# Reading two column tiles of a projection chunk out of one PSUM bank in a one-layer transformer trunk

## The chip, the core and the metric

One core of a Trainium2 chip runs the kernel. TensorE multiplies (PE in the profile), VectorE (DVE) and ScalarE (ACT) do elementwise work, GpSimd (POOL) small parts of it, and SyncE (SP) issues the weight loads. TensorE writes its results to PSUM, eight banks of 128 partitions x 512 fp32 numbers. The metric is the device time of one execution in microseconds (us). Before the change the three timed runs took 469.76, 470.10 and 471.17 us.

## What is computed

The trunk has one layer for 256 tokens of width 1024: native sparse attention (NSA), a cross attention to 256 memory tokens, a convolutional feed-forward part, each behind an RMS norm with a residual. The change lies in the input projection of the first part:

```python
def nsa_mixer(h, w_in, pe_k, pe_v, ck_w1, ck_w2, cv_w1, cv_w2, w_out):
    q, kc, vc, ks, vs, kw, vw, gl = jnp.split(h @ w_in, cuts, axis=-1)
    ...
    k_cmp = _compress(kv(kc), pe_k, ck_w1, ck_w2)
    v_cmp = _compress(kv(vc), pe_v, cv_w1, cv_w2)
    ...   # 16 heads in 4 groups: compressed, selected and window attention, gated

def _compress(t, pe, w1, w2):      # blocks of 32 tokens, every 16 tokens
    ...
    return jax.nn.gelu(blk @ w1) @ w2
```

`q` has 1024 columns; `kc`, `vc`, `ks`, `kw` have 256 each.

## The kernel before

Every large product is done in pairs of fp32r numbers: a value is split into a high part (`hi`, rounded, on ScalarE) and a low part (`lo`, the rest, on VectorE), and `mm3` (L183 to L185) adds hi x hi, lo x hi and hi x lo in one PSUM bank. Weights come in chunks of 1 MB, each in two halves of 128 x 1024: SyncE loads a half into one of 4 `raw` buffers (L108), ScalarE writes `hi` (L116), VectorE writes `lo` (L120) and by that frees the `raw` buffer. There are 6 `hi` and 6 `lo` buffers. The chunks in order: w_vsvw (numbers 0 and 1), the compressed inputs w_kcvc (2 and 4), w_q (3, 11, 12, 13), w_ks (5), w_ck (6, 7), w_cv (8, 9), w_kw (10), then the memory keys (14 and on).

The front of the kernel (`first`, then `fill`) multiplies the normed input `hT` with these chunks. Each chunk has 256 columns, that is two column tiles of 128, and each tile takes 24 matmuls of 128 x 256 (`proj_ws_steps`). A tile's result fills half a bank, 128 x 256. Before the change each tile has a bank of its own, tagged "proj" or "S" (two banks each), and when its matmuls are done its `out` generator is put on a list that moves a step forward with each matmul group:

- `compress_in(j)`: VectorE multiplies the bank by `row`, the inverse norms (L430); ScalarE and VectorE split it into `c2` (four `c` on each engine for a tile, L188 and L192), and GpSimd copies parts of `c2` (L451, L453).
- `keys(br)`: VectorE multiplies by `row` into a spare part of `xT` (`scaled`, L411); ScalarE writes `KH` twice for each group of heads, VectorE `KL` (L477).
- `queries(ci)`: ScalarE writes half of `QS` (L578), VectorE the other (L584).

`hidden(j)` multiplies `c2` with the compression weights (`pM`, tag "S"), copies the result (`hsb`, L506), turns it by `pH` and computes the gelu; `compressed_keys` splits that into `gh` and `gl` and multiplies them in `pkc`. In the attention behind it, 32 head steps (scores `s`, softmax on VectorE and ScalarE, transposes `pt`, values `O`) are mixed with the last query chunks, the memory keys `pmk` and values `pmv`, and the first output products `pr_out`.

The code gives an order of priority. For TensorE, VectorE and ScalarE a scheduler with a time model makes the final order when the kernel is built; SyncE and GpSimd keep the order of the code.

Of the kernel before, what the change touches and what calls it, by code (L numbers as in the profile page):

```python
# [42 lines left out]
def trunk_kernel(ctx: ExitStack, tc: tile.TileContext, a, out):  # L43
    nc = tc.nc
# [16 lines left out]
    cc = const.tile([P, C_END], F32, name="cc")  # L61
# [118 lines left out]
    def mm3(ps, lw, rx, start, stop):  # L180

        (lh, ll), (rh, rl) = lw, rx
        nc.tensor.matmul(ps, lh, rh, start=start, stop=False)  # L183
        nc.tensor.matmul(ps, lh, rl, start=False, stop=False)  # L184
        nc.tensor.matmul(ps, ll, rh, start=False, stop=stop)  # L185

    def split_hi(hi, src, scale=None):
        nc.scalar.activation(hi, src, AF.Copy, scale=1.0 if scale is None else scale)  # L188

    def split_lo(lo, hi, src, scale=None):  # L190
        if scale is None:
# [79 lines left out]
    def act_pair(nm, tag, pool=act):  # L271
        return tuple(pool.tile([P, KT, S], F32R, tag=f"{tag}_{x}", name=f"{nm}_{x}") for x in ("hi", "lo"))
# [24 lines left out]
    def later(work):  # L297
        running.append(work)
# [19 lines left out]
    done = set()  # L318
# [10 lines left out]
    with tc.tile_pool(name="attn", bufs=1, reuse_waits="tile") as at:  # L329
        KH = at.tile([P, G, 2, 2, P], F32R, name="KH")  # L330
        KL = at.tile([P, G, 2, 2, P], F32R, name="KL")
# [8 lines left out]
        hT = act_pair("hT", "aA")  # L340

        xT = act.tile([P, KT, S], F32, tag="aB_hi", name="xT")
# [40 lines left out]
        QS = at.tile([P, G, HPG, S], F32R, name="QS")  # L383
        with tc.tile_pool(name="cmp", bufs=1, side="right", reuse_waits="tile") as cp:
# [24 lines left out]
            def scaled(ps):  # L409
                v = free.pop(0)  # L410
                nc.vector.tensor_tensor(v, ps[:, :S], row, op=ALU.mult)  # L411
                return v

            NB = 15
            NC = NB * G
            c2 = []

            def compress_in(j):  # L420
                B = [cp.tile([P, 8, 2, 64], F32R, name=f"c2{j}{i}") for i in range(2)]
                pe = cp.tile([P, 2, 8, 1], F32R, name=f"pe{j}")
                o = C_PE + j * 16
                nc.gpsimd.memset(f(B[1][:, :, :, NC + 1:64]), 0.0)
                c2.append(B)

                def out(m, ps):
                    yield from wait("row")
                    v = ps[:, :S]
                    nc.vector.tensor_tensor(v, v, row, op=ALU.mult)  # L430
                    if m == 0:
                        split((B[1][:, :, 0, NC], B[1][:, :, 1, NC], cc[:, o + 8:o + 16]),
                              (pe[:, 0, :, 0], pe[:, 1, :, 0], cc[:, o:o + 8]))
                    yield
                    items = []
                    for gp in range(2):
                        g = 2 * m + gp
                        for par in range(2):
                            v_ = v[gp * 64:gp * 64 + 64].rearrange(
                                "p (n jj r) -> p n jj r", jj=8, r=2)[:, :, :, par]  # L440
                            dh, dl = (B[0][par * 64:par * 64 + 64, :, x, :].rearrange(
                                "p jj (n g) -> p n jj g", g=G)[:, :, :, g] for x in range(2))
# [6 lines left out]
                    if m == 1:  # L449
                        for x in range(2):  # L450
                            nc.gpsimd.tensor_copy(B[1][:, :, x, 0:NC], f(B[0][:, :, x, G:16 * G]))  # L451
                        for x in range(2):
                            nc.gpsimd.tensor_copy(B[0][:, :, x, NC:NC + 1], f(pe[:, x]))  # L453
                        done.add(f"c2{j}")

                for m in range(2):
                    ps = bank(("proj", "S")[m], f"pc{j}{m}")
                    yield from proj_ws_steps(ps[:, :S], c_kv[j], m, hT)
                    later(out(m, ps))


            def keys(br):
                def out(m, ps):
                    yield from wait("row")
                    v = scaled(ps)
                    yield
                    items = []
                    for gp in range(2):
                        g = 2 * m + gp
                        own = slice(gp * 64, gp * 64 + 64)  # L470
                        oth = slice(64 - gp * 64, 128 - gp * 64)
                        v_ = v[own].rearrange("p (h k) -> p h k", h=2)
                        split_hi(KH[own, g, :, br, :], v_)
                        items.append((KH[own, g, :, br, :], KL[own, g, :, br, :], KH[oth, g, :, br, :], v_))
# [12 lines left out]
            gel = cp.tile([P, 2, 2, NC], F32, name="gel")  # L487
# [46 lines left out]
            for g in range(G):  # L534
                z = slice(64, 128) if g % 2 == 0 else slice(0, 64)
# [36 lines left out]
            def queries(ci):  # L572
                pr = ci // 2

                def out(i, ps):
                    for gp in range(2):
                        own = slice(gp * 64, gp * 64 + 64)
                        nc.scalar.activation(QS[own, 2 * pr + gp, i, :], ps[own, :S], AF.Copy, scale=0.125)  # L578
                    yield
                    for gp in range(2):  # L580
                        g = 2 * pr + gp
                        own = slice(gp * 64, gp * 64 + 64)
                        oth = slice(64 - gp * 64, 128 - gp * 64)
                        nc.vector.scalar_tensor_tensor(QS[oth, g, i, :], ps[own, :S], 0.125,  # L584
                                                       f(QS[own, g, i, :]), op0=ALU.mult,
                                                       op1=ALU.subtract)
# [362 lines left out]
    with tc.tile_pool(name="cross", bufs=1, reuse_waits="tile") as cr:  # L949
# [61 lines left out]
        for t in range(NT):  # L1011
            for ci in range(EARLY):
                ps = bank("proj", f"pcq{t}{ci}")
# [4 lines left out]
                for c in range(2):  # L1018
                    o = c * S + t * P
# [20 lines left out]
    with tc.tile_pool(name="ffn", bufs=1, reuse_waits="tile") as fp:  # L1040
# [8 lines left out]
        for t in range(NT):  # L1049
            for fi in range(FIRST):  # L1050
                ps = bank("proj", f"upt{t}{fi}")
# [4 lines left out]
                for gv_ in range(2):  # L1056
                    o = gv_ * S + t * P
# [158 lines left out]
```

## Time and profile before

| | us |
|---|---|
| median of 3 timed runs (lowest to highest) | 470.10 (469.76 to 471.17) |
| the profiled execution | 470.6 |
| its span, first to last instruction | 468.5 |
| TensorE busy | 449.5 |
| VectorE busy | 326.8 |
| ScalarE busy | 293.9 |
| GpSimd busy | 37.6 |

Busy times are of one profiled execution. Times within it count from the span's first instruction. A matmul's row lasts longer than the distance to the next one, since matmuls overlap: the pace is read from the starts. "Idle before" is the time that an engine stood still before an instruction, with what released it. The mean clock of TensorE over the whole execution was 0.986 of 2.4 GHz.

### The profile page before, as it was taken

To read this page: it belongs to the slowest core of one execution; us is meant where nothing else is said; L and a number is where in the kernel's file an instruction comes from. 1 tells how busy PE (TensorE), PEld (TensorE's weight loads), DVE (VectorE), ACT (ScalarE), POOL (GpSimd) and SP (SyncE) were. 2 spreads that over 40 slices of the span, in tenths; PEclk is the share of its full clock that TensorE was granted. 3 is DMA by queue.
4 is the path that set the end of the run, shared out by engine and by line. 5 is a ranking of instruction groups with operands and counts; after the bars stand their busy time and mean duration, and the time that the engine had idled before them with its cause. 6 is when DMAs were issued, how large, how long until landed. Compare 5 with 4: busy or idle time off the path is not lost.

```text
span 468.5 us, 8741 instructions
## 1 busy us (share of the span) xinstructions
PE 449.5 (96%) x3278; PEld 415.1 (89%) x3278; DVE 326.8 (70%) x716; ACT 293.9 (63%) x613; POOL 37.6 (8%) x82
## 2 busy tenths in 40 slices
PE   7999796999999999999999999999999999999994
PEld 3899695899999777899998899999999999888984
DVE  4779968688978697666455466987877777645413
ACT  5778858766778688675464466866555556534301
POOL 4122200301100000010000010000000000000103
PEclk8999988999999999999999999999999999999998
DMA  7986687434332201547325274755555555554402
GB/s 257 365 277 217 214 252 280 156 118 150 97 104 77 92 1 41 186 140 236 120 91 166 86 241 124 239 184 182 184 185 187 182 187 184 199 191 149 148 0 91
DMA packets 22074, 77.05 MB, mean 164 GB/s; under 512 B 2704, under 2 KB 3088, under 8 KB 22032
## 3 DMA queue, kind: packets, MB, share of 16 engines
q1 hardware_dynamic: 21312, 74.65, 48.1%
q10 hardware_dynamic: 720, 1.84, 1.2%
q8 instruction: 26, 0.43, 0.4%
q14 instruction: 16, 0.13, 0.1%
HBM read 75.43 MB, written 1.05 MB: 163 GB/s over the span
## 4 chain that ended last, share of the span: by engine, by line
PE 83%; DVE 6%; DMA 6%; ACT 2%; issue 2%; POOLq 0%; DVEq 0%; SPq 0%; POOL 0%; ACTq 0%
PE up L185 8%; PE up L184 8%; PE up L183 8%; PE pd L184 4%; PE pd L183 4%; PE pd L185 4%; DMA raw<-in_w_q 3%; DVE lo L120 3%; PE O L832 2%; PE pt L810 2%; PE pmk L183 2%; PE pcq L183 2%; PE pmk L184 2%; PE pmv L184 2%; PE pmv L183 2%
## 5 line engine op out<-in xcount | busy, mean ns | idle before, releaser
L120 DVE TENSOR_TENSOR lo<-raw,hi 128x1024 fp32r<-128x1024 f32 x134 | 164.0, 1229 | 67.8 <-ACT hi L116 66.9
L116 ACT ACTIVATE hi<-raw 128x1024 fp32r<-128x1024 f32 x134 | 141.6, 1059 | 64.4 <-PE pd L185 17.7
L183 PE MATMUL up<-h_hi,hi 128*128 128x256 f32 x304 | 86.2, 283 | 0.0
L185 PE MATMUL up<-h_hi,lo 128*128 128x256 f32 x304 | 86.1, 283 | 0.0
L184 PE MATMUL up<-h_lo,hi 128*128 128x256 f32 x304 | 86.1, 283 | 0.0
L183 PEld LDWEIGHTS up<-h_hi,hi 128*128 128x128 f32 x304 | 58.4, 192 | 0.0
L184 PEld LDWEIGHTS up<-h_lo,hi 128*128 128x128 f32 x304 | 58.4, 192 | 0.0
L185 PEld LDWEIGHTS up<-h_hi,lo 128*128 128x128 f32 x304 | 58.4, 192 | 0.0
L185 PE MATMUL pd<-hi,aT_lo 128*128 128x512 f32 (+1 forms) x110 | 38.5, 350 | 0.0
L184 PE MATMUL pd<-lo,aT_hi 128*128 128x512 f32 (+1 forms) x110 | 38.4, 349 | 0.0
L183 PE MATMUL pd<-hi,aT_hi 128*128 128x512 f32 (+1 forms) x110 | 38.4, 349 | 0.0
L796 ACT ACTIVATE pp<-pp,nm 128x128 f32<-128x128 f32 (+1 forms) x64 | 28.5, 447 | 6.1 <-DVE nm L790 5.4
L790 DVE CUSTOM_DVE_ANT_0 pp<-s,tri,nrs 128x128 f32<-128x128 f32 (+1 forms) x64 | 24.0, 413 | 5.2 <-PE pt L810 3.3
L185 PEld LDWEIGHTS pd<-hi,aT_lo 128*128 128x128 f32 x110 | 20.7, 188 | 3.0
L184 PEld LDWEIGHTS pd<-lo,aT_hi 128*128 128x128 f32 x110 | 20.7, 188 | 2.9
L183 PEld LDWEIGHTS pd<-hi,aT_hi 128*128 128x128 f32 x110 | 20.7, 188 | 2.9
L1076 ACT ACTIVATE th<-c 128x256 f32<-128x256 f32 x22 | 9.1, 414 | 22.2 <-DVE c L1074 22.2
L814 ACT ACTIVATE pT<-pt 128x256 f32<-128x256 f32 (+1 forms) x32 | 15.3, 485 | 11.2 <-PE pt L810 11.0
L183 PE MATMUL pq<-hT_hi,hi 128*128 128x256 f32 x64 | 19.0, 297 | 0.4 <-DVE QS L584 0.4
L185 PE MATMUL pq<-hT_hi,lo 128*128 128x256 f32 x64 | 19.0, 296 | 0.0
L184 PE MATMUL pq<-hT_lo,hi 128*128 128x256 f32 x64 | 18.9, 295 | 0.0
L804 DVE TENSOR_SCALAR pp<-pp,den 128x128 f32<-128x128 f32 (+1 forms) x64 | 18.4, 327 | 0.6
(305 smaller groups left out, 1146.7 us busy)
## 6 DMA issues: line engine op xcount, KB each, us to landing
raw<-in_w_up SPq DMA_DIRECT2D x44, 512.0 KB, 4.3
raw<-in_w_dn SPq DMA_DIRECT2D x20, 512.0 KB, 4.3
raw<-in_w_q SPq DMA_DIRECT2D x8, 512.0 KB, 6.1
raw<-in_w_mk SPq DMA_DIRECT2D x8, 512.0 KB, 5.0
raw<-in_w_mv SPq DMA_DIRECT2D x8, 512.0 KB, 3.8
raw<-in_w_out SPq DMA_DIRECT2D x8, 512.0 KB, 3.8
raw<-in_ca_wq SPq DMA_DIRECT2D x8, 512.0 KB, 4.5
raw<-in_ca_wo SPq DMA_DIRECT2D x8, 512.0 KB, 4.1
```

Source lines behind the costliest of these rows:

```text
L116: nc.scalar.activation(his[i][h], raws[i][h], AF.Copy)
L120: nc.vector.tensor_tensor(t, raws[i][h], f(his[i][h]), op=ALU.subtract)
L183: nc.tensor.matmul(ps, lh, rh, start=start, stop=False)
L184: nc.tensor.matmul(ps, lh, rl, start=False, stop=False)
L185: nc.tensor.matmul(ps, ll, rh, start=False, stop=stop)
L790: nc.vector.tensor_tensor_reduce(self.ppv[:, br], sv[:, br], tri[:, 1 - t:], nrs[:, t:t + 1], 3e38, ALU.add, ALU.min, self.nm[:, br:br + 1])
L796: nc.scalar.activation(self.ppv[:, br], self.ppv[:, br], AF.Exp, bias=self.nm[:, br:br + 1], scale=-1.0, accum_out=self.den[:, br:br + 1])
L804: nc.vector.tensor_scalar(self.ppv[:, br], self.ppv[:, br], den[:, br:br + 1], None, op0=ALU.mult)
L810: nc.tensor.transpose(self.pt[:, o:o + P], self.pp[:, o:o + P], ident)
L814: nc.scalar.activation(self.pT[:, :self.w], self.pt[:, :self.w], AF.Copy)
L832: nc.tensor.matmul(O[r:r + DK, m * P:(m + 1) * P], V[:, blk // 2, blk % 2, g, :], group[i].pT[:, blk * P:(blk + 1) * P], start=False, stop ...
L1076: nc.scalar.activation(th, c, AF.Tanh, scale=0.5)
```

## The change

A chunk's two column tiles now go into the two halves of one bank, and `out` runs once for the chunk, behind the second tile, on both halves: the compressed inputs are multiplied by `row` in one 128 x 512 instruction and split in four double `c` on each engine; the keys take a 512 wide part of `xT` at once; `KH`, `KL` and `QS` are written for both tiles in one instruction. The banks of the compressed inputs and the keys now all have the tag "S", those of the queries "proj". Multiplications and weights stay the same.

```diff
-            free = [xT[:, k] for k in range(1, KT)] * 2
+            free = [xT[:, k:k + 2] for k in (2, 4)]
...
-                def out(m, ps):
+                def out(ps):
                     yield from wait("row")
-                    v = ps[:, :S]
-                    nc.vector.tensor_tensor(v, v, row, op=ALU.mult)
...
+                    both = ps.rearrange("p (m s) -> p m s", m=2)
+                    nc.vector.tensor_tensor(both, both, row.unsqueeze(1).to_broadcast([P, 2, S]), op=ALU.mult)
...
+                ps = bank("S", f"pc{j}")
                 for m in range(2):
-                    ps = bank(("proj", "S")[m], f"pc{j}{m}")
-                    yield from proj_ws_steps(ps[:, :S], c_kv[j], m, hT)
-                    later(out(m, ps))
+                    yield from proj_ws_steps(ps[:, m * S:(m + 1) * S], c_kv[j], m, hT)
+                later(out(ps))
...
-                    v = scaled(ps)
+                    v = free.pop(0)
+                    nc.vector.tensor_tensor(v.rearrange("p a s -> p (a s)"), ps,
+                                            row.unsqueeze(1).to_broadcast([P, 2, S]), op=ALU.mult)
...
+                ps = bank("S", f"pk{br}")
                 for m in range(2):
-                    ps = bank(("S", "proj")[m], f"pk{br}{m}")
-                    yield from proj_ws_steps(ps[:, :S], c_ks if br == 0 else c_kw, m, hT)
-                    later(out(m, ps))
+                    yield from proj_ws_steps(ps[:, m * S:(m + 1) * S], c_ks if br == 0 else c_kw, m, hT)
+                later(out(ps))
...
-                        nc.scalar.activation(QS[own, 2 * pr + gp, i, :], ps[own, :S], AF.Copy, scale=0.125)
+                        nc.scalar.activation(QS[own, 2 * pr + gp, i:i + 2, :], both[own], AF.Copy, scale=0.125)
...
+                ps = bank("proj", f"pq{ci}")
                 for ct in range(2):
-                    ps = bank("proj", f"pq{ci}{ct}")
-                    yield from proj_ws_steps(ps[:, :S], c_q[ci], ct, hT)
-                    later(out((ci % 2) * 2 + ct, ps))
+                    yield from proj_ws_steps(ps[:, ct * S:(ct + 1) * S], c_q[ci], ct, hT)
+                later(out((ci % 2) * 2, ps))
```

The scheduler gives the three compute engines another order up to the end of the attention. VectorE has 714 rows of work in the old program and 690 in the new, ScalarE 531 and 507, TensorE 3154 in both. SyncE's and GpSimd's orders stay the same. In the lists `lo5_0` is the low part of the first half of chunk 5; before the change `pq11` is the second tile of query chunk 1, and after it `pq2` is the whole of query chunk 2.

VectorE from the first half of w_ks (chunk 5) to w_ck (chunk 6), before:

```order
L120 TENSOR_TENSOR lo5_0_367<-raw5_0_360,hi5_0_362 128x1024
L584 SCALAR_TENSOR_TENSOR QS_238<-pq00_359,QS_238 64x256 x2
L192 TENSOR_TENSOR c200_254<-pc00_258,c200_254 64x16x8 x4
L430 TENSOR_TENSOR pc11_507<-pc11_507,xT_102 128x256
L120 TENSOR_TENSOR lo5_1_385<-raw5_1_378,hi5_1_380 128x1024
L192 TENSOR_TENSOR c200_254<-pc01_333,c200_254 64x16x8 x4
L210 SCALAR_TENSOR_TENSOR sq_mem0b_1082,ss_mem0b_1081<-mem0_1045 128x512
L192 TENSOR_TENSOR c210_462<-pc11_507,c210_462 64x16x8 x4
L120 TENSOR_TENSOR lo6_0_476<-raw6_0_467,hi6_0_469 128x1024
```

After:

```order
L120 TENSOR_TENSOR lo5_0_366<-raw5_0_359,hi5_0_361 128x1024
L120 TENSOR_TENSOR lo5_1_384<-raw5_1_377,hi5_1_379 128x1024
L192 TENSOR_TENSOR c200_254<-pc0_258,c200_254 64x2x16x8 x4
L210 SCALAR_TENSOR_TENSOR sq_mem0b_1031,ss_mem0b_1030<-mem0_999 128x512
L120 TENSOR_TENSOR lo6_0_461<-raw6_0_452,hi6_0_454 128x1024
L580 SCALAR_TENSOR_TENSOR QS_238<-pq0_358,QS_238 64x512 x2
L120 TENSOR_TENSOR lo6_1_481<-raw6_1_474,hi6_1_476 128x1024
L120 TENSOR_TENSOR lo7_0_531<-raw7_0_517,hi7_0_519 128x1024
```

The second half of w_ks follows the first, the two products of the second input are gone from here, and `QS` comes behind the first half of w_ck.

TensorE around the first matmul of `pkc`, before:

```order
L184 MATMUL pq11_965<-hT_lo_101,hi11_1_780 128x256
L185 MATMUL pq11_965<-hT_hi_100,lo11_1_784 128x256
L183 MATMUL pkc_850<-gh_816,w2h_820 128x60
L183 MATMUL pq20_1019<-hT_hi_100,hi12_0_799 128x256
L184 MATMUL pq20_1019<-hT_lo_101,hi12_0_799 128x256
```

After:

```order
L185 MATMUL pq2_973<-hT_hi_100,lo12_1_804 128x256
L183 MATMUL pq2_973<-hT_hi_100,hi12_1_796 128x256
L183 MATMUL pkc_817<-gh_783,w2h_787 128x60
L184 MATMUL pq2_973<-hT_lo_101,hi12_1_796 128x256
L185 MATMUL pq2_973<-hT_hi_100,lo12_1_804 128x256
```

Before, `pkc` stood between query chunks 1 and 2; now it stands behind 19 matmuls of chunk 2's first tile.

TensorE at the scores of head 17 (`s200`), before:

```order
L779 MATMUL s200_1841<-KH_92,QS_238 128x256
L780 MATMUL s200_1841<-KL_93,QS_238 128x256
L183 MATMUL pmv11_2357<-hi19_0_1850,memT_hi_1009 128x256
L184 MATMUL pmv11_2357<-lo19_0_1874,memT_hi_1009 128x256
L185 MATMUL pmv11_2357<-hi19_0_1850,memT_lo_1010 128x256
```

After:

```order
L775 MATMUL s200_1785<-KH_92,QS_238 128x256
L776 MATMUL s200_1785<-KL_93,QS_238 128x256
L185 MATMUL pmv11_2301<-hi19_1_1854,memT_lo_964 128x256
L183 MATMUL pr_out00_2427<-hi20_0_1993,oT_hi_965 128x512
L184 MATMUL pr_out00_2427<-lo20_0_2004,oT_hi_965 128x512
L185 MATMUL pr_out00_2427<-hi20_0_1993,oT_lo_966 128x512
```

Before, the memory values (`pmv11`) still had 18 matmuls to go at head 17; now one is left, and the output products (`pr_out00`) begin there.

## Rows read from the trace of the kernel before

**Rows 1.** The page: span, and part 1, busy time of each engine.
```profile
span 468.5 us, 8741 instructions
PE 449.5 (96%) x3278; PEld 415.1 (89%) x3278; DVE 326.8 (70%) x716; ACT 293.9 (63%) x613; POOL 37.6 (8%) x82
```

**Rows 2.** Stretches: busy us (instructions) per engine, granted clock, DMA share, GB/s.
```profile
30.00:40.00 10.00, 10.00 (x86) 10.00 (x86) 9.15 (x20) 9.73 (x21) 2.81 (x7) 1.00 0.74 251
40.00:50.00 10.00, 10.00 (x86) 10.00 (x85) 9.79 (x19) 8.72 (x18) 1.46 (x3) 1.00 0.80 248
50.00:60.00 10.00, 6.39 (x48) 5.58 (x47) 9.09 (x15) 7.41 (x13) 1.15 (x2) 0.99 0.66 210
60.00:70.00 10.00, 10.00 (x73) 10.00 (x73) 6.74 (x13) 5.70 (x8) 0.00 (x0) 0.84 0.82 240
70.00:80.00 10.00, 5.56 (x35) 5.28 (x34) 8.01 (x17) 8.61 (x21) 0.00 (x0) 0.84 0.80 304
148.00:160.00 12.00, 12.00 (x90) 10.34 (x91) 7.65 (x34) 7.50 (x20) 0.00 (x0) 1.00 0.31 108
160.00:182.00 22.00, 20.70 (x168) 16.30 (x165) 20.18 (x106) 19.04 (x70) 0.22 (x1) 1.00 0.00 1
```

**Rows 3.** TensorE in order of time: start, us, work, [idle before <- releaser].
```profile
46.53 0.28 PE L499 MATMUL pM<-hi,c 128*128 128x256 f32 x1
...
59.39 0.44 PE L510 MATMUL pH<-ident,hsb 128*128 128x128 f32 x2 [1.95 <-ACT hsb L506]
...
71.95 0.28 PE L184 MATMUL pq<-hT_lo,hi 128*128 128x256 f32 x1
72.07 0.28 PE L185 MATMUL pq<-hT_hi,lo 128*128 128x256 f32 x1
76.43 0.30 PE L183 MATMUL pkc<-gh,w2h 128*128 128x60 f32 x1 [4.08 <-ACT gh L188]
77.09 0.55 PE L183 MATMUL pq<-hT_hi,hi 128*128 128x256 f32 x1 [0.36 <-DVE QS L584]
```

**Rows 4.** VectorE in order of time, 30 to 42 us.
```profile
30.60 1.23 DVE L120 TENSOR_TENSOR lo<-raw,hi 128x1024 fp32r<-128x1024 f32 x1 [0.36 <-ACT hi L116]
...
35.03 1.23 DVE L120 TENSOR_TENSOR lo<-raw,hi 128x1024 fp32r<-128x1024 f32 x1
...
37.79 0.69 DVE L210 SCALAR_TENSOR_TENSOR sq_mem0b<-mem 128x512 bf16<-128x512 f32 x1
...
40.18 2.36 DVE L120 TENSOR_TENSOR lo<-raw,hi 128x1024 fp32r<-128x1024 f32 x2
```

**Rows 5.** SyncE: its longest wait in total (us, times, longest); three weight loads.
```profile
SPq L108 <- DVE lo L120: 204.2, 75, 29.4
...
36.28 0.33 SPq L108 DMA_DIRECT2D raw<-in_w_ck  x1
...
41.43 0.33 SPq L108 DMA_DIRECT2D raw<-in_w_cv  x1
...
54.68 10.77 SPq L108 DMA_DIRECT2D raw<-in_w_q  x6
```

**Rows 6.** ScalarE in order of time, before `gh`.
```profile
72.73 1.06 ACT L116 ACTIVATE hi<-raw 128x1024 fp32r<-128x1024 f32 x1 [1.17 <-DMA raw<-in_w_q]
73.69 1.70 ACT L188 ACTIVATE KH<-xT 64x256 fp32r<-64x256 f32 x4
```

**Rows 7.** By line and form: count, busy us, mean ns, idle; VectorE, then ScalarE.
```profile
L584 DVE SCALAR_TENSOR_TENSOR QS<-pq,QS 64x256 fp32r<-64x256 f32 x16 | 6.8, 422 | 3.1 <-ACT QS L578 2.9
L192 DVE TENSOR_TENSOR c<-pc,c 64x128 fp32r<-64x128 f32 x16 | 6.3, 391 | 0.4 <-ACT c L188 0.2
L936 DVE TENSOR_TENSOR x_sb<-pr_wo,x_sb 128x512 f32<-128x512 f32 x4 | 2.7, 687 | 5.1 <-PE pr_wo L185 5.1
...
L578 ACT ACTIVATE QS<-pq 64x256 fp32r<-64x256 f32 x16 | 6.0, 375 | 1.1 <-PE pq L185 0.9
L708 ACT ACTIVATE sT<-pst 64x512 f32<-64x512 f32 x4 | 2.4, 588 | 0.3 <-PE pst L702 0.3
```

More of the change, by code (lines that the diff above doesn't have):

```diff
@@ L407, in rms @@
                 nc.gpsimd.tensor_scalar(hrs, rs_x, 0.5, None, op0=ALU.mult)
[L409 to L412, printed above, removed]
             NB = 15
@@ L425, in compress_in @@
                 c2.append(B)
-                def out(m, ps):
+                def out(ps):
                     yield from wait("row")
-                    v = ps[:, :S]
-                    nc.vector.tensor_tensor(v, v, row, op=ALU.mult)
-                    if m == 0:
-                        split((B[1][:, :, 0, NC], B[1][:, :, 1, NC], cc[:, o + 8:o + 16]),
-                              (pe[:, 0, :, 0], pe[:, 1, :, 0], cc[:, o:o + 8]))
+                    both = ps.rearrange("p (m s) -> p m s", m=2)
+                    nc.vector.tensor_tensor(both, both, row.unsqueeze(1).to_broadcast([P, 2, S]), op=ALU.mult)
+                    split((B[1][:, :, 0, NC], B[1][:, :, 1, NC], cc[:, o + 8:o + 16]),
+                          (pe[:, 0, :, 0], pe[:, 1, :, 0], cc[:, o:o + 8]))
                     yield
@@ L436, in out @@
                     for gp in range(2):
-                        g = 2 * m + gp
                         for par in range(2):
-                            v_ = v[gp * 64:gp * 64 + 64].rearrange(
-                                "p (n jj r) -> p n jj r", jj=8, r=2)[:, :, :, par]
+                            v_ = ps[gp * 64:gp * 64 + 64].rearrange(
+                                "p (m n jj r) -> p m n jj r", m=2, jj=8, r=2)[:, :, :, :, par]
                             dh, dl = (B[0][par * 64:par * 64 + 64, :, x, :].rearrange(
-                                "p jj (n g) -> p n jj g", g=G)[:, :, :, g] for x in range(2))
+                                "p jj (n m gp) -> p m n jj gp", m=2, gp=2)[:, :, :, :, gp] for x in range(2))
                             items.append((dh, dl, v_))
@@ L448, in out @@
                         split_lo(lo, hi, v_)
[L449 to L454, printed above, removed]
+                    for x in range(2):
+                        nc.gpsimd.tensor_copy(B[1][:, :, x, 0:NC], f(B[0][:, :, x, G:16 * G]))
+                    for x in range(2):
+                        nc.gpsimd.tensor_copy(B[0][:, :, x, NC:NC + 1], f(pe[:, x]))
+                    done.add(f"c2{j}")
+                ps = bank("S", f"pc{j}")
                 for m in range(2):
-                    ps = bank(("proj", "S")[m], f"pc{j}{m}")
-                    yield from proj_ws_steps(ps[:, :S], c_kv[j], m, hT)
-                    later(out(m, ps))
+                    yield from proj_ws_steps(ps[:, m * S:(m + 1) * S], c_kv[j], m, hT)
+                later(out(ps))
             def keys(br):
-                def out(m, ps):
+                def out(ps):
                     yield from wait("row")
-                    v = scaled(ps)
+                    v = free.pop(0)
+                    nc.vector.tensor_tensor(v.rearrange("p a s -> p (a s)"), ps,
+                                            row.unsqueeze(1).to_broadcast([P, 2, S]), op=ALU.mult)
                     yield
@@ L468, in out @@
                     for gp in range(2):
-                        g = 2 * m + gp
                         own = slice(gp * 64, gp * 64 + 64)
                         oth = slice(64 - gp * 64, 128 - gp * 64)
-                        v_ = v[own].rearrange("p (h k) -> p h k", h=2)
-                        split_hi(KH[own, g, :, br, :], v_)
-                        items.append((KH[own, g, :, br, :], KL[own, g, :, br, :], KH[oth, g, :, br, :], v_))
+                        v_ = v[own].rearrange("p m (h k) -> p m h k", h=2)
+                        hi, lo, copy = (z[r].rearrange("p (m gp) h b k -> p m gp h b k", gp=2)[:, :, gp, :, br]
+                                        for z, r in ((KH, own), (KL, own), (KH, oth)))
+                        split_hi(hi, v_)
+                        items.append((hi, lo, copy, v_))
                     yield
@@ L575, in out @@
                 def out(i, ps):
+                    both = ps.rearrange("p (i s) -> p i s", i=2)
                     for gp in range(2):
                         own = slice(gp * 64, gp * 64 + 64)
-                        nc.scalar.activation(QS[own, 2 * pr + gp, i, :], ps[own, :S], AF.Copy, scale=0.125)
+                        nc.scalar.activation(QS[own, 2 * pr + gp, i:i + 2, :], both[own], AF.Copy, scale=0.125)
                     yield
@@ L583, in out @@
                         oth = slice(64 - gp * 64, 128 - gp * 64)
-                        nc.vector.scalar_tensor_tensor(QS[oth, g, i, :], ps[own, :S], 0.125,
-                                                       f(QS[own, g, i, :]), op0=ALU.mult,
+                        nc.vector.scalar_tensor_tensor(QS[oth, g, i:i + 2, :], both[own], 0.125,
+                                                       f(QS[own, g, i:i + 2, :]), op0=ALU.mult,
                                                        op1=ALU.subtract)
+                ps = bank("proj", f"pq{ci}")
                 for ct in range(2):
-                    ps = bank("proj", f"pq{ci}{ct}")
-                    yield from proj_ws_steps(ps[:, :S], c_q[ci], ct, hT)
-                    later(out((ci % 2) * 2 + ct, ps))
+                    yield from proj_ws_steps(ps[:, ct * S:(ct + 1) * S], c_q[ci], ct, hT)
+                later(out((ci % 2) * 2, ps))
             def compressed_keys():
```

## Prediction

> **What bounds the kernel now.** I read the page first: the profiled execution spans 468.5 us and TensorE is busy for 449.5 of them [rows 1]. So nearly all of the span is matmul time, the change removes no matmul, and only TensorE's idle time and its slow stretches can be won. Next the table of stretches, to see where those lie [rows 2]. From 30 to 50 us TensorE is busy throughout, from 50 to 60 it is busy for 6.39 us, from 70 to 80 for 5.56, and in 60 to 70 and 70 to 80 the granted clock averages 0.84. A mean of 0.84 over 10 us is 3.2 us at the lower of the two levels, 1.2 GHz, which throws away up to 1.6 us of matmul work each time. So about 8 us of idle time and up to 3 us of slow clock lie between 50 and 80 us, exactly the stage that the change rewrites. Everything after 190 us keeps its order.
>
> Then the two large waits of TensorE [rows 3]. One ends at 59.39 (1.95 us, the copy `hsb`). The other starts behind the matmul of 72.07 and ends at 76.43: 4.08 us, until ScalarE has written `gh`, the high part of the compressed keys' hidden layer, which `pkc` multiplies. Behind `pkc` the third query chunk then waits 0.36 us more, for VectorE to empty the bank (`QS`).
>
> Why is `gh` late? On ScalarE it stands behind four `KH` copies, and these behind a split that waited 1.17 us for the last half of w_q to land [rows 6]. That load left SyncE late: the six w_q halves go out between 54.68 and 65.45, and what SyncE waits for is VectorE's `lo`, 204.2 us in total [rows 5], because a `raw` buffer is free only when `lo` has read it. VectorE's rows show the same link from its side: `lo` of 35.03 ends at 36.26 and a load leaves at 36.28; the first `lo` of 40.18 ends at 41.4 and a load leaves at 41.43 [rows 4, 5]. VectorE is busy for 9.15, 9.79 and 9.09 us of each 10 from 30 to 60 [rows 2]. So VectorE's queue paces the weights here, and TensorE pays at 50 to 80.
>
> **The change part by part.** *Fewer, larger instructions.* By the order, VectorE and ScalarE lose 24 instructions each: 2 row products of the compressed inputs, 8 `c` splits, 2 products for the keys, 4 `KL` and 8 `QS` on VectorE; 8 `c`, 8 `KH` and 8 `QS` on ScalarE. Two 64x256 `QS` on VectorE cost 2 x 0.422 = 0.844, and the nearest form of twice the size, 128x512 from a bank, 0.687: 0.157 saved for each instruction removed. On ScalarE 2 x 0.375 - 0.588 = 0.162 [rows 7]. So 24 x 0.157 = 3.8 us and 24 x 0.162 = 3.9 us go from the two queues. The strided `c` splits in double size are not in the trace: one costs at least the 0.391 of the single one and at most two of them, 0.78; I take 2 x 0.391 - 0.157 = 0.63.
>
> The Trainium skill (Perfetto Trace Analysis, Optimizing Scalar/DVE Operations) gives smaller overheads, about 125 ns for VectorE on PSUM and 60 on SBUF; the rows' 0.157 is used. By these figures the 20 removed instructions on PSUM and 4 on SBUF are worth an estimated 2.7 us, and the forecast below would be some 0.5 us higher.
>
> *VectorE's order.* The `lo` of the second w_ks half now stands right behind the first. It can end at 30.60 + 2 x 1.23 = 33.06 instead of 36.26, so its buffer's load leaves 3.2 us earlier [rows 4, 5]. The next `lo` has four double `c` (2.5 us) and a 0.69 square ahead of it and ends at 33.06 + 2.5 + 0.7 + 1.2 = 37.5 instead of 41.4. The lead then shrinks: the second input's `c` splits now come all four together behind the second memory square, and `KL` moves ahead of a `lo`. Adding durations down both queues in the new order, the six w_q loads leave between 0.5 and 2.2 us earlier. Nothing earlier than that can reach `gh`; if the transfers themselves set the pace (0.80 of the DMA engines' time in 70 to 80 [rows 2]), it is 0. I take **1.6 us**, the later w_q halves being nearer the upper end.
>
> *TensorE's order at `pkc`.* The third query chunk has its own bank now, so it needn't wait for the second chunk's bank, and 19 of its matmuls stand ahead of `pkc`. They run at 0.12 us each (71.95 to 72.07 [rows 3]): 19 x 0.12 = **2.3 us** of work that fills the wait. In the old order that chunk waited for the bank alone behind `pkc`, not for weights. The **0.4 us** wait for the bank goes as well. If the cover is gone, because TensorE arrives late by as much as `gh` is early, the 1.6 us is lost but the 2.3 stays.
>
> *Bank sharing.* The five tiles pc, pk, pM now all take turns in two banks. `pM0` started at 46.53 [rows 3]; its bank is that of the second compressed input, whose last split I put at 47.0 by the same addition. That is a wait of about 0.5 us, and 2 us if the second memory square, which stands ahead of the splits on ScalarE, gets its load late. TensorE still has 3.6 us of idle time to come in 50 to 60 [rows 2] behind it, on weights that don't depend on `pM0`, so I cost it at nothing. One step stands against me there: `pH1` now follows two matmuls that need the first w_q half. That wait may grow by some 2 us, but 12 more matmuls (1.4 us) are done before it.
>
> *The attention's order.* The scheduler moved this too. The memory projections (288 matmuls) fill gaps between the heads; before head 17's scores 270 of them stood, now 287, and with transposes 21 more instructions in all. At 0.12 us that is 2.5 us of TensorE's work taken out of the second half of the heads, where only the softmax engines are left to set the pace. From 148 to 160 VectorE is busy 7.65 of 12 us, from 160 to 182 20.18 of 22 [rows 2]: idle 4.35 and 1.82. The softmax can move up into the first, hardly in the second. Bounds: nothing is lost, or all 2.5. I take half, **1.2 us**.
>
> **Sum:** 2.3 + 0.4 + 1.6 - 1.2 = 3.1, say 3 us off a span of 468.5. The profiled execution took 470.6 us in all and the three timed runs have a median of 470.1, 0.5 below it. So 470.1 - 3.0 = **467.1 us**.
>
> **The rivals.**
>
> *More.* If TensorE no longer comes to a standstill at `pkc`, the second stretch at half clock (1.6 us) may go too, and the heads may give nothing back: 2.3 + 0.4 + 1.6 + 1.6 = 5.9, less some waiting left over, 464.6. For it: the clock fell only behind the two large waits. Against: I still see up to 2.3 us of wait.
>
> *Given back.* The softmax engines set the pace from head 17 on, and w_q is early by only 0.5: 2.3 + 0.4 + 0.5 - 2.5 = 0.7, which is 469.4. For it: 20.18 of 22 us.
>
> *The shared bank.* `pM0` waits 2 us for the second input's splits and everything behind them on ScalarE and VectorE is late with it, so that w_q gains nothing: 2.3 + 0.4 - 1.2 = 1.5, which is 468.6. Against: the idle time that follows takes most of it. The Trainium skill (Perfetto Trace Analysis, Matmuls) says that independent groups should rotate through banks so that emptying one overlaps the next; this rival is what that rule would do here.
>
> *Slower.* In the tail without projections TensorE stands still between heads and its clock falls. Before, 160 to 182 holds only 1.3 us of its idle time and the clock stays at 1.00 [rows 2]. With 2.5 us less of its work between the heads, a pause like the one that ended at 59.39 [rows 3], behind which the clock fell, becomes possible. Each costs 1.6 us as above; two of them give 2.3 + 0.4 + 0.5 - 2.5 - 3.2 = -2.5, which is 472.6. It decides from the second such pause on, since with one the sum is -0.9. Against: 20.7 of 22 us are busy there now.
>
> That the change doesn't do what it says can be ruled out: the order shows the double forms and the counts.
>
> **How the numbers follow.** Forecast 0.50, more 0.17, given back 0.15, shared bank 0.07, slower 0.11. A measurement of this kernel tells about 0.3% from no change, which is 1.4 us. The forecast with its own spread (465.6 to 468.9) and "more" give faster 0.68; "given back" and most of the shared bank are the same, with the forecast's upper edge 0.21; slower 0.11. The range from 464.5 to 470.4 takes in everything but the slower case and the far end of "more".
>
> **What would show it.** In the profile after: VectorE's double forms near 0.69 and the `c` form near 0.63; the `lo` that ended at 36.26 ending near 33; the w_q loads leaving 0.5 to 2.2 us earlier; no wait of the third query chunk for `QS`, and a wait of TensorE at `pkc` under 2.3 us; first scores about 3 to 4 us earlier, and the attention's end about 3 us earlier. If the waits at 50 to 80 us shrink and the total doesn't move, my tail term is wrong; if `pkc` comes no earlier than 76 us, the DMA and not VectorE paced w_q.

## The result and the profile after

Four runs of the changed kernel took 463.66 to 464.90 us, median 463.88, beside a median of 469.93 for the kernel before: a ratio of 0.989, 95% interval 0.987 to 0.991. By the medians it is faster by 6.0 us, by the ratio by 5.2 (4.1 to 6.3), where 3.0 was forecast, and the median lies 0.6 us below the low end of the range. Six more runs of the same kernel in a later measurement, below, gave 465.76 and 0.993 (0.990 to 0.995), which is inside the range. So the change is worth some 3.5 to 6 us.

The profiled execution after took 463.8 us. First the page: the span, and the busy time of each engine.

```profile
span 461.9 us, 8682 instructions
PE 445.3 (96%) x3278; PEld 411.5 (89%) x3278; DVE 325.1 (70%) x692; ACT 289.0 (63%) x589; POOL 41.8 (9%) x82
```

TensorE is busy for 4.2 us less than in [rows 1] with the same 3278 matmuls. No matmul was removed, so most of this is matmul time that ran at the lower clock before: the two stretches at 0.84 in [rows 2] make up to 3.2 us of it (2 x 0.16 x 10). The table of stretches (columns as in [rows 2]) shows where:

```profile
40.00:50.00 10.00, 8.21 (x67) 7.83 (x66) 9.27 (x16) 6.54 (x11) 2.50 (x4) 1.00 0.63 204
50.00:60.00 10.00, 8.76 (x73) 8.36 (x72) 8.68 (x13) 7.72 (x13) 0.00 (x0) 1.00 0.78 244
60.00:70.00 10.00, 10.00 (x86) 10.00 (x85) 6.84 (x12) 5.22 (x7) 0.00 (x0) 1.00 0.91 299
70.00:80.00 10.00, 8.34 (x70) 8.14 (x70) 8.56 (x17) 9.85 (x22) 0.00 (x0) 1.00 0.51 197
...
90.00:100.00 10.00, 8.95 (x67) 7.75 (x65) 8.42 (x26) 5.90 (x14) 3.41 (x4) 1.00 0.36 122
...
160.00:182.00 22.00, 20.68 (x141) 16.35 (x140) 18.89 (x77) 18.00 (x51) 0.22 (x1) 1.00 0.10 29
```

The granted clock was 0.84 in two of these stretches before; now it is 1.00 in all. From 70 to 80 us TensorE gets 70 matmuls done where it got 35. TensorE in order of time (start, duration, work, [idle before <- releaser]), its three largest waits and what stands ahead of `pkc`:

```profile
47.91 0.36 PE L494 MATMUL pM<-hi,c 128*128 128x256 f32 x1 [1.45 <-DVE c L192]
...
71.38 0.28 PE L183 MATMUL pq<-hT_hi,hi 128*128 128x256 f32 x1
73.31 0.29 PE L183 MATMUL pkc<-gh,w2h 128*128 128x60 f32 x1 [1.66 <-ACT gh L188]
73.45 0.36 PE L184 MATMUL pq<-hT_lo,hi 128*128 128x256 f32 x1
...
91.24 0.70 PE L244 MATMUL pb_mem<-dg_mem 128*128 128x256 f32 x2 [1.05 <-POOL dg_mem L243]
```

The stop at `pkc` is 1.66 us instead of 4.08 [rows 3], chunk 2 is at work on both sides of it, and its wait for `QS` is gone. Two new stops stand there: `pM0` waits 1.45 us for the last split of the bank that it shares, and `pb_mem` 1.05 us for GpSimd. Both matter below.

### The profile page after: what moved, and what is told of

The parts are those of the page before. It is cut to its first block, busy times and chain, and to the rows that moved or that the text cites. A ratio compares the mean times of both kernels' runs of the same rounds, so it can differ in the third digit from the quotient of the medians.

```text
span 461.9 us, 8682 instructions
## 1 busy us (share of the span) xinstructions
PE 445.3 (96%) x3278; PEld 411.5 (89%) x3278; DVE 325.1 (70%) x692; ACT 289.0 (63%) x589; POOL 41.8 (9%) x82
## 3 DMA queue, kind: packets, MB, share of 16 engines
HBM read 75.43 MB, written 1.05 MB: 166 GB/s over the span
## 4 chain that ended last, share of the span: by engine, by line
PE 89%; DVE 4%; DMA 2%; ACT 1%; POOL 1%; issue 1%; POOLq 0%; DVEq 0%; SPq 0%; ACTq 0%
PE up L183 8%; PE up L185 8%; PE up L184 8%; PE pd L185 4%; PE pd L183 4%; PE pd L184 4%; PE O L828 3%; PE pt L806 2%; DVE lo L120 2%; PE pcq L183 2%; PE pmv L185 2%; PE pmv L184 2%; PE pmv L183 2%; PE pcq L185 2%; PE pcq L184 2%; PE pr_out L183 2%
## 5 line engine op out<-in xcount | busy, mean ns | idle before, releaser
L184 PE MATMUL pmv<-lo,memT_hi 128*128 128x256 f32 x64 | 18.7, 292 | 0.0
L183 PE MATMUL pmk<-memT_hi,hi 128*128 128x256 f32 x64 | 18.2, 285 | 0.2 <-DVE QS L580 0.2
```

## Where the time went: one table for all kernels

Executions start differently: the first matmul of `pc` came at 21.00 us in the profiled run before, at 20.23 after, and between 19.31 and 22.62 in the others. What the kernels do to the time is therefore counted from that matmul, between starts in the trace: to the first matmul of `pkc` that reads `gh`, from there to the last of `pq`, and on to the last of `pr_out`. Behind that all take 263.6 us to the last matmul, but for two with 264.0 and 264.1.

| kernel (label) | ratio to before, 95% interval | to `pkc` | to last `pq` | to last `pr_out` | sum |
|---|---|---|---|---|---|
| before | | 55.43 | 17.66 | 104.56 | 177.65 |
| after | 0.989 (0.987 to 0.991) | 53.09 | 12.87 | 105.87 | 171.83 |
| after_again | 0.993 (0.990 to 0.995) | 53.27 | 12.87 | 107.39 | 173.53 |
| q_only | 0.988 (0.984 to 0.992) | 52.82 | 12.95 | 105.37 | 171.14 |
| c_only | 0.998 (0.996 to 1.001) | 55.63 | 16.60 | 103.89 | 176.12 |
| a_q2 | 1.000 (0.998 to 1.002) | 55.25 | 18.71 | 104.56 | 178.52 |
| a_c2 | 0.990 (0.988 to 0.993) | 53.04 | 12.88 | 105.85 | 171.77 |
| small | 0.995 (0.993 to 0.997) | 58.50 | 12.48 | 104.53 | 175.51 |
| q20S | 0.998 (0.996 to 1.001) | 54.17 | 18.35 | 104.15 | 176.67 |
| fill6 | 0.998 (0.996 to 1.001) | 54.74 | 16.87 | 104.57 | 176.19 |
| rot | 0.992 (0.988 to 0.995) | 55.14 | 15.88 | 105.09 | 176.11 |
| b_ghv | 0.997 (0.995 to 0.998) | 52.24 | 18.98 | 104.14 | 175.35 |
| a_ghv | 0.988 (0.985 to 0.992) | 52.97 | 12.66 | 105.30 | 170.93 |
| q_ghv | 0.987 (0.984 to 0.989) | 51.36 | 13.99 | 105.48 | 170.83 |

So of the 6.6 us between the two profiled spans 0.8 is the start, and 5.8 the change: 2.3 to `pkc`, 4.8 behind it, and 1.3 given back in the attention.

My theory then (A): TensorE no longer stops at `pkc`, it has work there and keeps its clock. The rival (B): the lighter queues of VectorE and ScalarE gain in proportion to the instructions removed.

## Experiments: which part of the change

**q_only**, the kernel before with the queries part alone:

```diff
...
+                ps = bank("proj", f"pq{ci}")
                 for ct in range(2):
-                    ps = bank("proj", f"pq{ci}{ct}")
-                    yield from proj_ws_steps(ps[:, :S], c_q[ci], ct, hT)
-                    later(out((ci % 2) * 2 + ct, ps))
+                    yield from proj_ws_steps(ps[:, ct * S:(ct + 1) * S], c_q[ci], ct, hT)
+                later(out((ci % 2) * 2, ps))
```

> The kernel before with the queries part alone: both column tiles of a query chunk in one bank, QS written in half as many instructions (8 fewer on VectorE, 8 on ScalarE). By the order, 18 matmuls of query chunk 2 stand ahead of the first pkc matmul here, as after the whole change. Theory A (the gain comes from TensorE no longer stopping at pkc: 19 x 0.12 us of work moved ahead, the bank wait gone, and the clock not falling behind the stop): most of the whole change's 6 us, 464 to 466.5 us, and a granted clock of 1.00 in 70 to 80 us. Theory B (the gain is the lighter VectorE and ScalarE queues, in proportion to the instructions removed, 8 of 24): 6 x 8/24 = 2.0 us, 468 us, and the stop at pkc stays over 3 us.

It took 462.84 us, less than theory A's range: the whole gain, by a third of the removed instructions.

**a_q2**, the reverse: the kernel after with this part undone.

> The kernel after with the queries part undone: each query tile again has a bank of its own and QS is written per tile; compressed inputs and keys stay merged. By the order, no matmul of query chunk 2 stands ahead of pkc. Theory A: 468 to 469.5 us, the wait at pkc over 3 us and the half clock behind it back. Theory B: 16 of 24 removed instructions stay removed, 6 x 16/24 = 4 us, 465.9 us.

It took 469.28 us, ratio 1.000: nothing is gained by the other two parts, though 32 of the 48 instructions stay removed. **c_only**, the compressed inputs alone:

> The kernel before with the compressed inputs part alone: one bank for a chunk's two tiles, one row product and four double splits (10 fewer instructions on VectorE, 8 on ScalarE). By the order, no matmul of query chunk 2 stands ahead of pkc, as before the change. Theory A: the stop at pkc and the half clock behind it stay, so at most the 0.5 to 1.6 us by which gh comes earlier: 468.3 to 469.5 us, clock 0.84 in one of the stretches 60 to 80. Theory B: 6 x 10/24 = 2.5 us, 467.4 us.

468.19 us, and the interval includes no change. **a_c2**, the kernel after with the compressed inputs undone:

> The kernel after with the compressed inputs part undone: queries and keys stay merged, the compressed inputs are again multiplied and split per tile in banks of their own (proj and S). By the order, 18 matmuls of query chunk 2 stand ahead of pkc. If the order at pkc and the clock carry the gain: 462.5 to 464.5. If the gain goes with the number of removed instructions: 10 of 24 less on VectorE, 469.5 - 3.4 = 466.1.

465.44 us, above the first case's range and nearer to the second's 466.1, so that the time decides nothing here; the stages are those of after to 0.1 us, and in this profile the first `pc` came 2.0 us later than in after's. Theory B falls with q_only (462.84, it had 468) and a_q2 (469.28, it had 465.9). TensorE at `pkc` in q_only, then in a_q2, and a_q2's stretch from 70 to 80 us:

```profile
72.48 0.29 PE L183 MATMUL pkc<-gh,w2h 128*128 128x60 f32 x1 [1.37 <-ACT gh L188]
```
```profile
74.56 0.42 PE L183 MATMUL pkc<-gh,w2h 128*128 128x60 f32 x1 [5.07 <-ACT gh L188]
...
70.00:80.00 10.00, 5.20 (x24) 5.10 (x24) 8.37 (x18) 9.84 (x21) 0.00 (x0) 0.70 0.55 218
```

a_q2's TensorE comes to `pkc` early, stops for 5.07 us, and goes on at half clock. Its lighter queues did bring w_q sooner (ScalarE starts on the last half 50.69 us behind the first `pc`, 51.73 before), but ScalarE's order spends that again. ScalarE in a_q2:

```profile
70.01 1.06 ACT L116 ACTIVATE hi<-raw 128x1024 fp32r<-128x1024 f32 x1 [1.90 <-DMA raw<-in_w_q]
70.97 2.56 ACT L188 ACTIVATE KH<-xT 64x512 fp32r<-64x512 f32 x4
73.43 0.75 ACT L573 ACTIVATE QS<-pq 64x256 fp32r<-64x256 f32 x2
74.21 0.30 ACT L188 ACTIVATE gh<-gel 128x120 fp32r<-128x120 f32 x1
```

From that `hi` to `gh` it is 4.20 us here and 3.35 before (72.73 [rows 6] to 76.08): the four doubled `KH` and still a tile's `QS` stand ahead of `gh`. In the kernel after no `QS` does:

```profile
69.41 1.06 ACT L116 ACTIVATE hi<-raw 128x1024 fp32r<-128x1024 f32 x1 [1.50 <-PE pq L185]
70.38 2.56 ACT L188 ACTIVATE KH<-xT 64x512 fp32r<-64x512 f32 x4
72.96 0.30 ACT L188 ACTIVATE gh<-gel 128x120 fp32r<-128x120 f32 x1
73.17 1.18 ACT L574 ACTIVATE QS<-pq 64x512 fp32r<-64x512 f32 x2
```

## Experiments: what in the queries part does it

**q20S**: work ahead of `pkc` by a bank alone, all instructions in their old size.

```diff
-                    ps = bank("proj", f"pq{ci}{ct}")
+                    ps = bank("S" if (ci, ct) == (2, 0) else "proj", f"pq{ci}{ct}")
```

> The kernel before with one word changed: the first tile of query chunk 2 takes its bank from the tag S instead of proj. All instructions keep their old size. By the order, 26 matmuls of query chunk 2 now stand ahead of the first pkc matmul. If the gain is that TensorE has work (and keeps its clock) while it waits for gh: 463 to 465 us, as with the queries part alone (462.8). If the merged QS instructions carry a share of it by themselves: 466 to 468. If neither: 469.5.

468.76 us, no gain that can be told from none: I had expected 463 to 465. TensorE in order of time, and its stretch from 80 to 90 us:

```profile
74.78 0.30 PE L183 MATMUL pkc<-gh,w2h 128*128 128x60 f32 x1 [1.11 <-ACT gh L188]
...
81.86 0.55 PE L183 MATMUL pq<-hT_hi,hi 128*128 128x256 f32 x1 [2.77 <-DVE QS L584]
...
80.00:90.00 10.00, 8.14 (x47) 7.10 (x48) 8.78 (x19) 6.95 (x18) 3.87 (x5) 0.66 0.46 158
```

The stop at `pkc` shrank as in the kernel after, and another came 7 us later: chunk 3's first tile waits 2.77 us for the bank of chunk 1's second tile, whose `QS` stand behind eight splits of the memory on both engines (on VectorE they ran from 80.85 to 81.71). The clock fell behind this stop instead (0.66). Theory A as I put it was thus too short: moving work ahead of `pkc` isn't enough, the next bank must be free as well. In the kernel after, one `QS` step takes both tiles of chunk 1 out of their bank at once, ahead of the memory's splits (from 73.17 on ScalarE, to 75.77 on VectorE), and chunk 3 waits for nothing.

**small**: the banks and the single `out` of the kernel after, with every instruction in its old size.

```diff
-                    nc.vector.tensor_tensor(both, both, row.unsqueeze(1).to_broadcast([P, 2, S]), op=ALU.mult)
+                    for m in range(2):
+                        nc.vector.tensor_tensor(both[:, m], both[:, m], row, op=ALU.mult)
...
+                    items = [tuple(z[:, m] for z in it) for m in range(2) for it in items]
...
```

> The kernel after with its banks and its generators (one bank for two tiles, out once behind the second tile), but every row product, split, KH, KL and QS instruction in the old size and number, two where after has one. By the order, 21 matmuls of query chunk 2 stand ahead of pkc. Theory A (where the banks let TensorE go decides, not the size of the instructions): 464 to 466 us. Theory B (instruction overhead decides): no faster than before, 469 to 471 us. A mixture would lie at 466 to 468.

466.59 us, a mixture: half the gain. TensorE:

```profile
52.85 0.55 PE L498 MATMUL pM<-hi,c 128*128 128x256 f32 x1 [6.78 <-DVE c L192]
...
78.35 0.30 PE L183 MATMUL pkc<-gh,w2h 128*128 128x60 f32 x1 [0.37 <-ACT gh L188]
```

Here the shared bank bites: `pM0` waits 6.78 us where it waited 1.45 in after, and `pkc` comes 3.1 us later than before. Yet the work from `pkc` on is as short as after (12.48), so that the sum still falls. Only 1.2 us of the longer wait is the size of the `c`: eight took 3.16 us on ScalarE and 3.14 on VectorE, four double ones 2.60 and 2.49 in after. More of it is order, since the two row products of the second input stand apart on VectorE and ScalarE waits for the second. VectorE, then ScalarE in small:

```profile
42.97 0.43 DVE L426 TENSOR_TENSOR pc<-pc,xT 128x256 f32<-128x256 f32 x1
43.31 2.35 DVE L120 TENSOR_TENSOR lo<-raw,hi 128x1024 fp32r<-128x1024 f32 x2
...
45.91 0.42 DVE L426 TENSOR_TENSOR pc<-pc,xT 128x256 f32<-128x256 f32 x1
...
46.37 3.16 ACT L188 ACTIVATE c<-pc 64x128 fp32r<-64x128 f32 x8 [2.92 <-DVE pc L426]
```

A merged row product can't be taken apart like this. How small would do with its row products side by side was not run. The Trainium skill (Perfetto Trace Analysis, Matmuls) says that independent matmul groups should rotate through banks, so that emptying one overlaps the next group's matmuls; the trace agrees that sharing has a price, 6.78 us of waiting here and 1.45 in after.

**fill6**: the clock by itself. Six matmuls whose result is overwritten keep TensorE at work during the stop in the kernel before.

```diff
                 pkc = bank("PT", "pkc")
+                for _ in range(6):
+                    nc.tensor.matmul(pkc[0:NC, :S], gel[:, 0, 0], xT[:, 0], start=True, stop=True)
```

> The kernel before with six more matmuls (60x256, fp32) whose result is overwritten: they read the compressed keys' gelu and stand on TensorE right behind query chunk 1, ahead of the first pkc matmul, so that TensorE works through most of the 4.1 us stop; six at some 0.46 us each (two rows of a pb matmul, 94.22 to 94.46, taken twice) make 2.8 us. The rest of the order is the same, but for one split of the memory input. No useful work is moved. If the clock's fall behind the stop is a cost of its own: the clock stays at 1.00 from 70 to 80, and the time falls by up to half of the 3.9 us at 1.2 GHz, 1.9 us, to 467.6 (468.5 if half of the runs have no such fall anyway). If only the idle time counts: 469.5, no change.

468.35 us, ratio 0.998 (0.996 to 1.001): by the time alone inconclusive. The trace says more. TensorE, and two stretches:

```profile
72.65 2.80 PE L603 MATMUL pkc<-xT,gel 128*60 128x256 f32 x12
77.36 0.30 PE L183 MATMUL pkc<-gh,w2h 128*128 128x60 f32 x1 [1.91 <-ACT gh L188]
...
70.00:80.00 10.00, 7.72 (x53) 6.23 (x51) 7.29 (x16) 8.77 (x19) 0.00 (x0) 1.00 0.85 318
80.00:90.00 10.00, 9.60 (x80) 8.23 (x79) 9.79 (x21) 9.43 (x25) 3.16 (x6) 1.00 0.41 136
```

The clock stayed at 1.00, and the 96 `pq` matmuls behind `pkc` took 11.96 us from start to start instead of 13.34. So the fall behind `pkc` costs 1.4 us between these two executions; 0.6 of it went to `pst`, which then waited 0.4 for `KLc`, and the stage is 0.8 shorter. The earlier fall, at 60 us, was absent in this execution too and brought nothing: TensorE only stood still longer, 2.80 filled and 1.91 idle, 4.7 us where it was 4.08. (`pkc` came 0.7 us sooner all the same, but with the weights: the first w_q half landed in 5.78 us instead of 6.75, and ScalarE's `hi` waited for it in both.) In this kernel a fall ahead of a wait was paid out of the wait; only the one behind the last wait cost time.

## Experiments: the stops that are left

**b_ghv, a_ghv, q_ghv**: `gh` on VectorE right behind the gelu, in the kernels before, after and q_only.

```diff
-                split((gh, gl, gel[:, 0], 0.5))
+                nc.vector.tensor_scalar(gh, gel[:, 0], 0.5, None, op0=ALU.mult)
+                split_lo(gl, gh, gel[:, 0], 0.5)
```

> The kernel before with gh written by VectorE in the same way and nothing merged. gh is then there at 72 us instead of 76.4. If the stop of TensorE there hangs on gh alone: it goes, and the time falls by 4 us of idle time and 1.9 us of slow clock, to 464. If the bank of query chunk 1's tiles holds chunk 2 back as well (its QS are written at 75.3 to 76.9 behind the last KH copies): the stop stays nearly as long, now with QS as what ended it, the clock falls as before, and the time is 469 to 470.

467.50 us, between the two: `pkc` comes 3.2 us earlier than before, but the stop is partly moved. TensorE waits for `gl` and then for the bank, and the clock falls behind them (0.85 in 70 to 80):

```profile
74.20 0.30 PE L184 MATMUL pkc<-gl,w2h 128*128 128x60 f32 x1 [1.36 <-DVE gl L194]
75.67 0.36 PE L183 MATMUL pq<-hT_hi,hi 128*128 128x256 f32 x1 [0.73 <-DVE QS L584]
...
70.00:80.00 10.00, 7.91 (x55) 7.72 (x54) 9.30 (x22) 9.76 (x26) 0.00 (x0) 0.85 0.75 282
```

> The kernel after with gh, the high part of the compressed keys' hidden layer, written by VectorE right behind the gelu instead of by ScalarE behind the hi split of the last w_q half and four KH copies. The orders differ in four rows of TensorE, six of VectorE, five of ScalarE. If TensorE's stop at pkc (1.7 us) is what is left to win there, and it hangs on ScalarE's queue: the stop goes, the clock never falls there, 461.5 to 463 us, and runs lie closer together. If something else is late at the same time (query chunk 2's weights or its bank): the wait moves and the time stays at 463.9.

463.77 us, beside 465.76 for the kernel after in the same measurement; the intervals overlap, so that this gain is likely and not shown. The runs do not lie closer together, as expected, but further apart (461.90 to 466.71). The stop at `pkc` is gone, TensorE busy for 10.00 of 10 us from 70 to 80.

> The queries part alone (462.8 us) with gh written by VectorE. By the order, 11 matmuls of query chunk 2 stand ahead of pkc instead of 18. If the stop at pkc (1.4 us there) is all that is left: 461 to 462.5 us, the fastest of all. If TensorE then waits for the weights or the bank instead: 462.8, no change.

462.71 us (461.97 to 464.36). Its six runs all lie below the six of after_again (465.27 to 468.64) on the same chip: in this measurement a version that beats both kernels. Against q_only (462.84) it is no different.

**rot**: the second compressed input in a bank that `pM0` doesn't need.

```diff
-                ps = bank("S", f"pc{j}")
+                ps = bank(("S", "proj")[j], f"pc{j}")
```

> The kernel after with the second compressed input in a bank of the tag proj, so that pM0 no longer needs the bank that its splits empty at 47.8 us; the order of the three compute engines is the same word for word. If the 1.45 us wait of pM0 costs time: it goes, and the time falls by up to 1.45 us to 462.4. If the idle time behind it absorbs it, as the prediction had it: the wait moves to the next weight half or to pkc, and the time stays at 463.9 within 0.3%.

466.28 us, ratio 0.992, above both expected times. `pM0` starts 1.1 us earlier, counted from the first `pc`, and the kernel is no faster than after in either measurement, as the prediction had it. But in this profile `gh` was 2 us later with the same order of instructions, so that a small gain could be hidden under it. ScalarE:

```profile
65.83 1.06 ACT L116 ACTIVATE hi<-raw 128x1024 fp32r<-128x1024 f32 x1 [0.28 <-DMA raw<-in_w_q]
66.80 0.29 ACT L521 ACTIVATE u<-u 128x120 f32<-128x120 f32 x1
70.88 1.06 ACT L116 ACTIVATE hi<-raw 128x1024 fp32r<-128x1024 f32 x1 [3.79 <-DMA raw<-in_w_q]
```

Counted from the first `pc`, the second w_q half left 0.6 us later than after and took 5.66 us to land instead of 4.65; its `raw` buffer was free later by as much, and the last half left 1.6 us later. TensorE then stopped for 3.05 us at `pkc`, and the clock fell (0.74 from 70 to 80). Whether the other bank or chance made the transfer slower is open.

**after_again**, to see how much of this varies:

> The kernel after once more, unchanged, beside other kernels of this call: the spread of its runs and whether the stop at pkc is long enough in some of them for the clock to fall. If the clock term is part of its gain in every run: 463 to 465 us and no half clock between 40 and 90 us in the profile. If the fall comes and goes with the landing of the last w_q half, as the kernel with the second compressed input in the other tag's bank suggests (gh late by 2 us with the same order, 466.3): some runs at 466, and a median of 464 to 466.

465.76 us. No fall behind `pkc` here, but one behind `pb_mem`, which in the first profile had the same stop and no fall:

```profile
90.83 0.70 PE L244 MATMUL pb_mem<-dg_mem 128*128 128x256 f32 x2 [1.06 <-POOL dg_mem L243]
...
90.00:100.00 10.00, 9.17 (x54) 7.75 (x55) 7.20 (x20) 5.53 (x13) 2.15 (x4) 0.83 0.27 89
```

That execution's attention is 1.5 us longer (107.39 to 105.87). It is the one large difference between the two profiles of the kernel after (0.2 us to `pkc` and 0.5 behind `pr_out` are the others), so the 3.5 and the 6.0 us of the two measurements are at least in part this fall. The mean clocks of the other runs say the same: 0.990 to 0.998 in the four of the first measurement, 0.983 to 0.991 in these six, with a mean of 0.988, and 0.989 in the 17 runs of the kernel before beside them. The 3.5 us came without a higher mean clock than before, and the rest of the 6.0 with one. In q_only and q_ghv `pb_mem` waits 0.68 and 0.31 us, and the attention is 0.4 to 0.5 shorter than after.

## Why the prediction was half right

**Fewer, larger instructions: right.** By line and form (count, busy us, mean ns, idle), after:

```profile
L580 DVE SCALAR_TENSOR_TENSOR QS<-pq,QS 64x512 fp32r<-64x512 f32 x8 | 5.5, 689 | 1.0 <-ACT QS L574 0.8
L188 ACT ACTIVATE c<-pc 64x256 fp32r<-64x256 f32 x8 | 5.1, 638 | 0.1
L192 DVE TENSOR_TENSOR c<-pc,c 64x256 fp32r<-64x256 f32 x8 | 5.0, 622 | 1.7 <-ACT c L188 1.7
```

0.687 was taken for `QS` and 0.63 for `c`; 0.689, 0.638 and 0.622 came. Added up over the merged groups, VectorE has 3.7 us less and ScalarE 4.2 (3.8 and 3.9 forecast). By itself that gained nothing, as a_q2 shows.

**w_q earlier: right in size, in part by luck, and by a longer way than I thought.** The lists of VectorE and SyncE after, beside [rows 4, 5]:

```profile
29.83 2.36 DVE L120 TENSOR_TENSOR lo<-raw,hi 128x1024 fp32r<-128x1024 f32 x2 [0.42 <-ACT hi L116]
```
```profile
52.37 10.56 SPq L108 DMA_DIRECT2D raw<-in_w_q  x6
```

The `lo` of the second w_ks half ends at 32.19 (36.26 before; 33.06 expected, and the start was 0.8 earlier). The last w_q half left 1.75 us earlier counted from the first `pc` (62.60 and 65.12 us in the spans), where 1.6 was taken from 0.5 to 2.2. But all six were to lie in that range, and they left 1.54 earlier, 0.49 later, and 0.74, 0.54, 2.66 and 1.75 earlier. The last took 0.8 less to land (6.70 and 7.50 us), which makes the 2.3 at `pkc`. VectorE alone doesn't pace these loads: ScalarE's `hi` waited for landings, 1.17 us in [rows 6]. What I hadn't seen is that this needs the queries part too: in a_q2 and c_only `QS` ahead of `gh` eats it. And q_only came to its 2.6 us at `pkc` otherwise: its last half left only 0.24 us earlier, landed in 5.79 us instead of 7.50, and no `QS` stood ahead of `gh` (2.69 us from that `hi` to `gh`, 3.35 before). The last half took 4.11 to 7.77 us to land over the fourteen profiles; what makes the difference was not tested, so that this part of the gain is explained only down to the transfer.

**19 matmuls ahead of `pkc`, and the bank: right**, 2.3 and 0.4 us; the wait for `QS` is gone. q20S shows that the two belong together: the first without the bank behind it gains nothing.

**The clock: the step that failed.** The forecast left both slow stretches as they were, at 0 gain, since up to 2.3 us of wait was still in sight; the rival "more" had it. 1.66 us were left, and the clock did not fall: 1.4 us by fill6, 1.8 by the mean of 0.90 from 76.43 to 94.10 us before. The front then adds up: 2.3 + 2.3 + 0.4 + 1.4 to 1.8 + 0.4 for four transposes (`psc`) that moved behind the last `pq` = 6.8 to 7.2, against 7.1 in the table, where 4.3 was forecast. The first slow stretch, which I would have counted at the same price, was worth nothing. Nor is the clock won in every run: in after_again the same price came back behind `pb_mem`, and there the gain was 3.5 us where 3.0 was forecast.

**The tail: right in size (1.2 forecast, 1.3 measured) by luck, wrong in place.** The softmax engines were to lose TensorE's cover behind head 17. TensorE's idle time from 140 to 200 us is 1.58 us, 1.30 before; the heads gave back 0.3. From the last `pq` to the last `pr_out` TensorE stood still for 2.86 us, 1.30 before; the largest part of that is the stop at `pb_mem`, 1.05, which no step of mine had. Its busy time fell from 103.26 to 103.01 us although the four transposes, 0.4, came in; why is open. At `pb_mem`, with the front shorter, GpSimd's norm of the memory ends last, and GpSimd's own rows were longer. After, then before:

```profile
86.85 1.03 POOL L218 TENSOR_SCALAR ms_mem<-ss_mem1a 128x1 f32<-128x1 f32 x1
88.93 2.26 POOL L243 TENSOR_SCALAR dg_mem<-ident,rs_m 128x128 f32<-128x128 f32 x2
```
```profile
89.04 0.22 POOL L218 TENSOR_SCALAR ms_mem<-ss_mem1a 128x1 f32<-128x1 f32 x1
90.31 1.22 POOL L243 TENSOR_SCALAR dg_mem<-ident,rs_m 128x128 f32<-128x128 f32 x2
```

No run was made on what lengthens them.

**The shared bank: underestimated and harmless.** 0.5 us expected, 1.45 measured; the load of the second memory half did come late, ScalarE waited 2.17 us for it, so that the case named for 2 us applied in part. Without it, rot was no faster.

**Slower: did not come**; the clock is 1.00 from 140 to 200 us in the kernel after.

Of the cases, "more" (464.6) is nearest to the first measurement; the second (465.8) lies between it and the forecast.

## What to carry to other kernels

Judge a merged instruction by the order that its buffers allow, not by the overhead that it saves: here two thirds of the merging gained nothing, and the third that let the next chunk's matmuls run past a wait into a free bank gained it all. Where a stop is shortened, look for the next bank that the moved work will need, and price the slow clock behind the stop with it, but only if no later wait absorbs it. Where tiles share a bank, merge its emptying too: shared and emptied in small instructions, it gave half, and the order drew the pair of row products apart.

## What the runs showed of the hardware that I had not expected

A stop of the same length at the same place did or did not bring the clock down. Behind `pM0`'s 1.44 to 1.45 us the clock stayed at 1.00 in the kernel after and fell to 1.2 GHz in after_again (0.92 from 40 to 50) and in a_ghv:

```profile
40.00:50.00 10.00, 7.52 (x54) 7.14 (x53) 9.30 (x16) 5.98 (x10) 2.49 (x4) 0.84 0.60 211
50.00:60.00 10.00, 10.00 (x73) 10.00 (x73) 8.49 (x12) 8.36 (x13) 0.00 (x0) 0.82 0.69 214
```

Likewise `pH1`: 1.95 us and a fall before [rows 2, 3], 1.90 us and none in fill6. So a profile of one execution shows whether a fall happened there, not whether it will. Runs of the kernel before spread from 466.7 to 472.1 us, and of the kernel after from 463.7 to 468.6.
